# The first weight sum of the last feed-forward product in a tile of the larger pool, a third tile finished by an accumulating store, and the last tile's gain product in two parts

## The chip, the cores and the metric

One core of a Trainium2 chip (trn2). The metric is the time of one execution on the device in microseconds (us); lower is better. Engines are named as the profile names them: PE (TensorE matmul) and PEld (its weight load), DVE (VectorE), ACT (ScalarE), POOL (GpSimd), SP (SyncE, which here only issues transfers).

## What is computed

One decoder layer over 1,024 tokens and 16 meta tokens, width 1,024, all in float32. The change lies in the last third of it, the feed-forward block and its norm:

```python
u = rmsnorm(h, g_pre_ffn[l])
f = jnp.square(jax.nn.relu(u @ w_ff1[l])) @ w_ff2[l]
h = h + rmsnorm(f, g_post_ffn[l])
return h[:, N_META:]
```

Here h is [1024, 1024] without the meta tokens, w_ff1 is [1024, 4096], w_ff2 is [4096, 1024], and rmsnorm(x, g) is x / sqrt(mean(x^2) + 1e-6) * g. Ahead of it stand the input projection, sliding-window attention, a linear recurrence and the output projection; the change leaves them alone.

## The kernel before

**Products in three matmuls.** To keep float32 accuracy each operand is split into a high part (a copy rounded by ACT, line 95) and a low part (source minus high part, by DVE, line 98). Each block product is then three matmuls: high times high (line 123), high times low (line 124), low times high (line 125), all accumulated in the same bank of PSUM. A tile of 128x1024 elements thus costs one ACT instruction and one DVE instruction before PE may use it.

**Seven products in place of eight.** Both feed-forward products are done in a Strassen-Winograd form: sums and differences of blocks on DVE or in transfers, seven block products in place of eight. For the second feed-forward matmul the list PLAN holds the seven products, i = 0 to 6. Each is done in eight steps q = 0 to 7 over the 4,096 hidden rows, and a step (i, q) needs one weight tile (128x1024, from one or two blocks of w_ff2) and one activation tile, both split. In each step PE runs 4 row tiles j times 6 matmuls. The seventh product (i = 6) is the last one; its weight is the sum of two blocks of w_ff2 and its activation is the difference of two activation blocks. Its row tile j = 3 is computed in two halves of 256 columns, in two PSUM banks. The last three steps (q = 5, 6, 7) are held back and run row tile by row tile at the end, so that the tiles j = 0, 1, 2, 3 are finished one after the other.

**Two ways of a weight sum.** `fetch_2` loads the blocks. Either both blocks come by plain loads on SP's queue (line 1058) and DVE adds them in `prep_2`, or the first comes by a plain load and the second by an accumulating transfer issued by POOL (line 1055), which adds it to the tile in flight. For i = 6 the list LASTW says, for each q, from which pool the tile comes and whether the second block has a tile of its own (a name) or is accumulated (None). The accumulated ones are q = 0, 2, 3, 5, 7.

**Pools.** A pool is a set of tiles that are given out again once all readers of the former content are done; a transfer into such a tile waits for them. "raw" and "e" have 2 tiles each and hold weights as loaded; "ws" has 4 (split weights); "b" has 17 (split activations, sums of activations, and, until product 5 is over, four result tiles); "a" has 16.

**Queues.** Every engine takes its instructions in the order of its own queue. A scheduler writes that order when the program is built, with a timing model of its own. POOL's queue holds few things: the accumulating transfers, and the powers -1/2 of a norm (`rstd_of`, lines 160 to 164: DVE writes ms, POOL raises it to -1/2 as rs at line 164, DVE multiplies by rs).

**The end.** The output tiles 4 to 7 (results "1", j = 0 to 3) are complete after product 5 and are finished by `finish_early` during the end of product 5 and the start of product 6: squares on ACT, ms, rs, one DVE instruction (line 1124), and a store on POOL that accumulates onto the residual already standing in the output (line 1128). The output tiles 0 to 3 are finished by `finish_half` and `finish_late`. For j = 0 and 1 the way is the same as in `finish_early` (squares of the last half on ACT, line 1117; ms; rs; line 1158; accumulating store, line 1162). For j = 2 and 3 the sum of squares is taken by DVE (line 1165), rs by POOL (line 1173), the product with the gain g by DVE (line 1175, the first half earlier at line 1145), and the residual, loaded ahead by SP (line 1143), is added by DVE together with the factor rs (line 1177); two plain stores by SP and ACT follow (line 1180).

Of the kernel before, what the change touches and what calls it, by code (L numbers as in the profile page):

```python
# [9 lines left out]
F32 = mybir.dt.float32  # L10
F32R = mybir.dt.float32r
AF = mybir.ActivationFunctionType
ALU = mybir.AluOpType
# [3 lines left out]
P = 128  # L17
# [20 lines left out]
def hybrid_layer(  # L38
# [6 lines left out]
    nc = tc.nc  # L45
# [4 lines left out]
    small = ctx.enter_context(tc.tile_pool(name="small", bufs=4))  # L50
# [7 lines left out]
    def slot(tag, shape, dt=F32):  # L58
        uid[0] += 1
        return slab.tile(shape, dt, tag=tag, name=f"{tag}{uid[0]}", bufs=bufs[tag])  # L60
# [44 lines left out]
    def behind(name, *inss):  # L105
        for ins in inss:
            tc.add_manual_dep(
                ins, name,
                mybir.DependencyInfo(
                    mybir.DependencyClass.NoSync, mybir.DependencyReason.DATA  # L110
                ),
                reason="order",
            )
# [38 lines left out]
    half_pow = const.tile([P, 1], F32, name="half_pow")  # L152
    nc.gpsimd.memset(half_pow, -0.5)

    def rstd_of(ssq_parts, n=P):
        ms = small.tile([P, 1], F32, name="ms", tag="ms")
        if len(ssq_parts) == 1:
            nc.gpsimd.tensor_scalar(ms[:n], ssq_parts[0], EPS, None, op0=ALU.add)
        else:
            nc.vector.scalar_tensor_tensor(  # L160
                ms[:n], ssq_parts[0], EPS, ssq_parts[1], op0=ALU.add, op1=ALU.add
            )
        rs = small.tile([P, 1], F32, name="rs", tag="rs")
        nc.gpsimd.tensor_tensor(rs[:n], ms[:n], half_pow[:n], op=ALU.pow)  # L164
        return rs[:n]
# [251 lines left out]
    for b in range(2):  # L417
        pv = bank("pt", (P, 4, P))
        for i in range(4):
            o = NMETA + (4 * b + i) * P  # L420
# [366 lines left out]
    def combine(dst, x0, x1, op):  # L787
        return nc.vector.tensor_tensor(dst, x0, x1, op=op).ins  # L788
# [227 lines left out]
    def product_by_parts(acc, w, op):  # L1016
# [22 lines left out]


    LASTW = [
        ("raw", None), ("e", "raw"), ("b", None), ("b", None), ("raw", "e"), ("b", None),
        ("e", "raw"), ("b", None),
    ]

# [67 lines left out]
    COLS = (slice(0, 512), slice(512, 1024))  # L1113

    def squares(sq, src, n):
        p_ = small.tile([P, 1], F32, name=f"sq{n}", tag=f"sq{n}")
        nc.scalar.activation(sq, src, AF.Square, scale=RMS_SC, accum_out=p_)
        return p_
# [13 lines left out]
    def finish_half(j):  # L1132

        o = slot("a", [P, D])
        acc, c = facc["0", j], COLS[1]
        ssq = small.tile([P, 1], F32, name=f"late{j}", tag=f"late{j}", bufs=1)
        nc.scalar.activation(
            o[:, c], acc[:, c], AF.Square, scale=RMS_SC, accum_out=ssq
        )
        h = None  # L1140
        if j > 1:
            h = slot("d", [P, D])
            nc.sync.dma_start(h, out[j * P : (j + 1) * P, :])
            nc.gpsimd.tensor_scalar(ssq, ssq, EPS, None, op0=ALU.add)
            behind(w_low[0], combine(o[:, c], acc[:, c], gffn_b[:, c], ALU.mult))
        halves[j] = h, o, ssq

    def finish_late(j, y, parts):

        h, o, ssq = halves[j]  # L1150
        acc = facc["0", j]
        for k, c in enumerate(parts):
            yield k
            ins = combine(acc[:, c], y[k], acc[:, c], ALU.add)
            if k == 1:
                behind(w_low[0], ins)
            if j < 2:
                w_low[0] = nc.vector.scalar_tensor_tensor(
                    o, acc, rstd_of([squares(o[:, c], acc[:, c], 0), ssq]), gffn_b,
                    op0=ALU.mult, op1=ALU.mult,  # L1160
                ).ins.name
                nc.gpsimd.dma_start(out[j * P : (j + 1) * P, :], o, accum_op=ALU.add)
                continue
            part = small.tile([P, 1], F32, name=f"part{k}", tag=f"part{k}")
            nc.vector.tensor_tensor_reduce(
                out=o[:, c], in0=acc[:, c], in1=acc[:, c], scale=RMS_SC * RMS_SC,
                scalar=ssq, op0=ALU.mult, op1=ALU.add, accum_out=part,
            )
            ssq = part
        if j < 2:  # L1170
            return
        rs = small.tile([P, 1], F32, name="rs", tag="rs")
        nc.gpsimd.tensor_tensor(rs, ssq, half_pow, op=ALU.pow)
        c = COLS[0]
        combine(o[:, c], acc[:, c], gffn_b[:, c], ALU.mult)
        for c, eng in zip(COLS[::-1], (nc.sync, nc.scalar)):
            w_low[0] = nc.vector.scalar_tensor_tensor(
                o[:, c], o[:, c], rs, h[:, c], op0=ALU.mult, op1=ALU.add
            ).ins.name
            eng.dma_start(out[j * P : (j + 1) * P, c], o[:, c])  # L1180
# [37 lines left out]
    for n, (i, q) in enumerate(steps):  # L1218
        while fetched < min(n + (4 if n < 45 else 6), len(steps)):
            raw_2[fetched] = fetch_2(fetched)  # L1220
            fetched += 1
        if n + 1 < len(steps):
            late = w_low[0]
            ready[n + 1] = prep_2(n + 1, "a" if n + 1 >= len(steps) - LAST else "ws")
        if q == 0:
            old = None if i == 0 else accs
            accs = [[bank(("acc", "s", "pt", "o")[j])] for j in range(4)]
            if i == 6:

                evict(5, 0, old[0][0], late)  # L1230
                accs[3] = [accs[3][0][:, :256], bank("acc")[:, :256]]
        if n < len(steps) - LAST:
            for j in range(4):
                for acc, cols in zip(accs[j], col_parts(i, j)):
                    step_mm(acc, j, q, ready[n], cols)
            del ready[n]
        if old and (q > 0 or i < 6) and q < 4:
            evict(i - 1, q, old[q][0], late)
        if i == 5 and q == 0:
            gffn_b = slot("a", [P, D])  # L1240
            nc.scalar.dma_start(gffn_b, g_post_ffn[0].partition_broadcast(P))
        if (i, q) in EARLY:
            finish_early(EARLY.index((i, q)))
        if i == 6 and 1 <= q < 5:
            finish_half(q - 1)
    for j in range(4):
        parts = col_parts(6, j)
        for k in finish_late(j, accs[j], parts):
            for n in sorted(ready):
                step_mm(accs[j][k], j, steps[n][1], ready[n], parts[k])  # L1250
# [31 lines left out]
```

## Time and profile before

| | us |
|---|---|
| median of 3 runs | 973.48 (972.43 to 975.89) |
| the profiled execution's own time | 972.95 |
| span of its profile, first to last instruction | 971.1 |
| mean granted clock of TensorE in it | 0.999 of full speed |

Times inside the span are counted from its start. A row of the timeline gives the start, the length of one instruction, the engine, the line of the kernel, the operation, what it writes and reads, and in brackets how long the engine was idle before it and what ended that. In the chain of work that ended last, each row is a start, a length and what the time was spent on; "issue" is time in which the engine waited for nothing that the profile shows. In the DMA view the last number of a row is the median time from issue to landing. Sums, differences and products of two tiles go through the helper `combine` and stand at its line 788. A window of the timeline may start with an instruction that began just before it.

### The profile page before, as it was taken

The page shows a single profiled execution, that of the slowest core. Times are in us where ns is not written, and L with a number is a line of the kernel's source. Part 1 is how long each engine was busy: PE and PEld are TensorE (multiplying, and loading weights), DVE is VectorE, ACT ScalarE, POOL GpSimd, SP SyncE. Part 2 cuts the span into 40 slices and gives each one's busy share as a digit, 9 for nine tenths or more (in the row PEclk, how much of TensorE's full clock was granted, in tenths as well). Part 3 has the DMA queues.
Part 4 walks back from the last instruction along what each step waited for, and adds up shares of the span by engine and source line. Part 5 has one row for each costly group of instructions (what it writes and reads, how often), then busy time and mean ns, then how long its engine had stood idle before and what let it go on. Part 6 is the DMA issues. An engine that isn't in the chain of part 4 may idle for free.

```text
span 971.1 us, 12490 instructions
## 1 busy us (share of the span) xinstructions
PE 953.7 (98%) x4782; PEld 803.0 (83%) x4782; DVE 674.6 (69%) x997; ACT 502.0 (52%) x809; POOL 82.4 (8%) x109
## 2 busy tenths in 40 slices
PE   6999999999999999999999999999999999999997
PEld 6999999888878887888888878888888888888786
DVE  6679997775976686665645465468557676779694
ACT  6646673567844554343555556555433344445350
POOL 4100000000002100000000000000111000003152
PEclk9999999999999999999999999999999999999999
DMA  9002001012234466576522264323678765548923
GB/s 296 23 1 66 23 23 44 23 48 64 84 119 144 159 207 209 173 251 209 198 87 87 97 206 125 114 87 114 172 176 198 186 224 187 184 163 195 223 80 87
DMA packets 88219, 130.13 MB, mean 134 GB/s; under 512 B 13624, under 2 KB 52552, under 8 KB 88160
## 3 DMA queue, kind: packets, MB, share of 16 engines
q1 hardware_dynamic: 79792, 107.33, 33.4%
q0 software_dynamic: 7792, 20.45, 10.1%
q10 hardware_dynamic: 576, 1.57, 0.4%
q8 instruction: 37, 0.61, 0.2%
q14 instruction: 22, 0.18, 0.1%
HBM read 110.46 MB, written 18.87 MB: 133 GB/s over the span
## 4 chain that ended last, share of the span: by engine, by line
PE 89%; DVE 4%; DMA 3%; issue 2%; ACT 1%; POOL 0%; SPq 0%; POOLq 0%; DVEq 0%; ACTq 0%
PE ps_acc L124 11%; PE ps_acc L123 11%; PE ps_acc L125 11%; PE ps_s L125 6%; PE ps_pt L123 6%; PE ps_s L124 6%; PE ps_pt L125 6%; PE ps_s L123 6%; PE ps_pt L124 6%; PE ps_o L124 5%; PE ps_o L123 5%; PE ps_o L125 5%; PE ps_o L506 2%; PE ps_pt L495 1%; DMA raw<-in_w_ff_dram 1%
## 5 line engine op out<-in xcount | busy, mean ns | idle before, releaser
L95 ACT CAST ws<-raw 128x1024 fp32r<-128x1024 f32 (+1 forms) x69 | 70.7, 1024 | 126.6 <-PE ps_o L124 48.8
L98 DVE TENSOR_TENSOR ws<-raw,ws 128x1024 fp32r<-128x1024 f32 (+1 forms) x70 | 83.5, 1194 | 59.6 <-ACT ws L95 59.5
L123 PE MATMUL ps_acc<-a,ws 128*128 128x256 f32 (+2 forms) x272 | 90.5, 333 | 0.6 <-DVE b L305 0.6
L124 PE MATMUL ps_acc<-a,ws 128*128 128x256 f32 (+2 forms) x272 | 89.8, 330 | 0.0
L125 PE MATMUL ps_acc<-a,ws 128*128 128x256 f32 (+2 forms) x272 | 89.4, 329 | 0.0
L98 DVE TENSOR_TENSOR b<-b,b 128x1024 fp32r<-128x1024 f32 (+2 forms) x48 | 57.6, 1201 | 24.7 <-PE ps_o L124 17.1
L95 ACT CAST ws<-e 128x1024 fp32r<-128x1024 f32 x43 | 45.0, 1046 | 55.3 <-PE ps_o L124 28.1
L95 ACT CAST b<-b 128x1024 fp32r<-128x1024 f32 (+2 forms) x48 | 49.4, 1030 | 42.8 <-DVE b L788 40.0
L98 DVE TENSOR_TENSOR ws<-e,ws 128x1024 fp32r<-128x1024 f32 x43 | 52.6, 1222 | 21.6 <-ACT ws L95 21.6
L123 PEld LDWEIGHTS ps_acc<-a,ws 128*128 128x128 f32 x272 | 51.2, 188 | 4.9 <-DVE b L305 0.8
L125 PEld LDWEIGHTS ps_acc<-a,ws 128*128 128x128 f32 x272 | 51.2, 188 | 4.6
L124 PEld LDWEIGHTS ps_acc<-a,ws 128*128 128x128 f32 x272 | 51.2, 188 | 3.9
L164 POOL TENSOR_TENSOR rs<-ms,half_pow 128x1 f32<-128x1 f32 (+1 forms) x31 | 21.3, 692 | 356.5 <-DVE ms L160 355.1
L123 PE MATMUL ps_acc<-ws,b 128*128 128x512 f32 (+1 forms) x120 | 46.3, 386 | 0.4 <-ACT ws L95 0.4
L124 PE MATMUL ps_acc<-ws,b 128*128 128x512 f32 (+1 forms) x120 | 46.5, 388 | 0.2 <-DVE ws L98 0.2
L125 PE MATMUL ps_acc<-ws,b 128*128 128x512 f32 (+1 forms) x120 | 46.2, 385 | 0.0
L123 PE MATMUL ps_pt<-ws,b 128*128 128x512 f32 x112 | 44.1, 394 | 0.0
L124 PE MATMUL ps_pt<-ws,b 128*128 128x512 f32 x112 | 44.1, 394 | 0.0
L125 PE MATMUL ps_pt<-ws,b 128*128 128x512 f32 x112 | 44.0, 393 | 0.0
L123 PE MATMUL ps_s<-ws,b 128*128 128x512 f32 x110 | 43.4, 395 | 0.0
L124 PE MATMUL ps_s<-ws,b 128*128 128x512 f32 x110 | 43.3, 393 | 0.0
L125 PE MATMUL ps_s<-ws,b 128*128 128x512 f32 x110 | 43.3, 393 | 0.0
(381 smaller groups left out, 2690.1 us busy)
## 6 DMA issues: line engine op xcount, KB each, us to landing
raw<-in_w_ff_dram SPq DMA_DIRECT2D x62, 512.0 KB, 4.0
e<-in_w_ff_dram SPq DMA_DIRECT2D x45, 512.0 KB, 3.6
d<-in_w_ff_dram SPq DMA_DIRECT2D x12, 512.0 KB, 3.8
s_dram<-d POOLq DMA_DIRECT2D x12, 512.0 KB, 3.9
raw<-in_w_in_dram SPq DMA_DIRECT2D x9, 512.0 KB, 3.6
c<-in_x_dram SPq DMA_DIRECT2D x8, 512.0 KB, 8.5
d<-in_x_dram SPq DMA_DIRECT2D x8, 512.0 KB, 4.6
out_dram<-raw SPq DMA_DIRECT2D x8, 512.0 KB, 2.6
```

What stands on the lines that cost most here:

```text
L95: nc.scalar.copy(hi, src)
L98: low = nc.vector.tensor_tensor(lo, src, f32(hi), op=ALU.subtract).ins
L123: nc.tensor.matmul(dst, lh, rh, start=start, stop=False, skip_group_check=True)
L124: nc.tensor.matmul(dst, lh, rl, start=False, stop=False, skip_group_check=True)
L125: nc.tensor.matmul(dst, ll, rh, start=False, stop=stop, skip_group_check=True)
L164: nc.gpsimd.tensor_tensor(rs[:n], ms[:n], half_pow[:n], op=ALU.pow)
L495: nc.tensor.transpose(pt[:, o : o + P], sn[h][:, 2 * bp + i, s * P : (s + 1) * P], ident,)
L506: nc.tensor.matmul(po[:, oc : oc + n], v, p_[:, pc : pc + n], start=first and k == 0, stop=last and k == 1, skip_group_check=True,)
```

## The change

Three edits. First, the weight tile of step (6, 0), the first weight sum of the last product, comes from the pool "b" and no longer from "raw"; it is still loaded by SP and then accumulated by POOL. Second, output tile 2 is finished as tiles 0 and 1 are (ACT squares, line 1158, accumulating store on POOL), so its residual is no longer loaded. Third, for tile 3 the product with g of the last 512 columns is made in two parts of 256 columns, inside the loop over the parts.

```diff
     LASTW = [
-        ("raw", None), ("e", "raw"), ("b", None), ("b", None), ("raw", "e"), ("b", None),
+        ("b", None), ("e", "raw"), ("b", None), ("b", None), ("raw", "e"), ("b", None),
         ("e", "raw"), ("b", None),
     ]
...
         h = None
-        if j > 1:
+        if j > 2:
             h = slot("d", [P, D])
...
-            if j < 2:
+            if j < 3:
                 w_low[0] = nc.vector.scalar_tensor_tensor(
...
             ssq = part
-        if j < 2:
+            if k == 1:
+                rs = small.tile([P, 1], F32, name="rs", tag="rs")
+                nc.gpsimd.tensor_tensor(rs, ssq, half_pow, op=ALU.pow)
+            combine(o[:, c], acc[:, c], gffn_b[:, c], ALU.mult)
+        if j < 3:
             return
-        rs = small.tile([P, 1], F32, name="rs", tag="rs")
-        nc.gpsimd.tensor_tensor(rs, ssq, half_pow, op=ALU.pow)
-        c = COLS[0]
-        combine(o[:, c], acc[:, c], gffn_b[:, c], ALU.mult)
```

The scheduler writes the queues anew. POOL's queue around the first weight sums, in the order of the two programs (the names are ours: sum q is the accumulating transfer of step (6, q); rs 7 and store 7 belong to output tile 7):

```
before: store 6, sum 2, rs 7, sum 3, store 7, sum 0, sum 5, sum 7
after:  store 6, sum 0, sum 2, rs 7, store 7, sum 3, sum 5, sum 7
```

On SP's queue, before: the plain load of sum 2, e (step (5, 7)), of sum 3, of sum 0, e, of sum 5, raw. After: the plain load of sum 0, e (step (5, 7)), of sum 2, of sum 3, raw, e, of sum 5, raw. On DVE's queue the order from the activations of step (5, 0) up to the end of product 6 is the same, but for one early product with g that is gone; at the very end, tile 2's line 1158 stands between tile 3's first addition of a PSUM bank (line 1154) and tile 3's first sum of squares, and tile 3's first product with g stands behind the addition of its second bank and ahead of the second sum of squares.

## The prediction

> **What bounds the kernel now.** I read the page first, then the chain of waits over the last 130 us, then the timelines of POOL, DVE and PE there.
>
> ```profile
> PE 953.7 (98%) x4782; PEld 803.0 (83%) x4782; DVE 674.6 (69%) x997; ACT 502.0 (52%) x809; POOL 82.4 (8%) x109
> PE 89%; DVE 4%; DMA 3%; issue 2%; ACT 1%; POOL 0%; SPq 0%; POOLq 0%; DVEq 0%; ACTq 0%
> ```
>
> PE is the bound: busy 98%, 89% of the chain. The change leaves its matmuls as they are, so it can only move PE's waits and the tail behind its last matmul. Near the edit the chain leaves PE:
>
> ```profile
> 889.74 5.08 DMA b<-in_w_ff_dram
> 894.86 6.88 issue
> 901.78 0.62 POOL b L1055
> ...
> 903.91 3.76 issue
> 907.68 9.19 DMA raw<-in_w_ff_dram
> 916.96 1.05 ACT ws L95
> 918.03 1.24 DVE ws L98
> 919.31 0.50 PE ps_acc L124
> ```
>
> Read upwards: PE waited for the split of the first weight sum (raw), whose accumulating transfer was issued only at 907.68. PE's rows give the price:
>
> ```profile
> 917.25 0.40 PE L125 MATMUL ps_o<-ws,b 128*128 128x512 f32 x1
> ...
> 918.39 0.40 PE L123 MATMUL ps_s<-ws,b 128*128 128x512 f32 x1
> 918.62 0.40 PE L123 MATMUL ps_pt<-ws,b 128*128 128x512 f32 x1
> 918.86 0.28 PE L123 MATMUL ps_o<-ws,b 128*128 128x256 f32 x1
> 919.31 0.50 PE L124 MATMUL ps_acc<-ws,b 128*128 128x512 f32 x1 [0.18 <-DVE ws L98]
> 919.65 0.40 PE L125 MATMUL ps_acc<-ws,b 128*128 128x512 f32 x1
> ```
>
> Undisturbed starts lie 0.23 apart for 512 columns (918.39 to 918.62) and half of it for 256. From 917.25 to 919.65 there should be five times 0.23 and one 0.12, 1.27; there are 2.40. The stall costs 1.13 us, and that is all that the first edit can gain.
>
> **Why was that sum late?** POOL's timeline:
>
> ```profile
> 890.11 0.89 POOL L1128 DMA_DIRECT2D out_dram<-a  x1 [2.53 <-DVE a L1124]
> 892.44 1.21 POOL L1055 DMA_DIRECT2D b<-in_w_ff_dram  x1 [1.44 <-issue]
> 893.19 1.45 POOL L164 TENSOR_TENSOR rs<-ms,half_pow 128x1 f32<-128x1 f32 x1
> 901.75 1.23 POOL L1055 DMA_DIRECT2D b<-in_w_ff_dram  x1 [7.11 <-PE ps_o L125]
> 902.51 1.41 POOL L1128 DMA_DIRECT2D out_dram<-a  x1
> 907.68 1.22 POOL L1055 DMA_DIRECT2D raw<-in_w_ff_dram  x1 [3.77 <-issue]
> 917.20 1.20 POOL L1055 DMA_DIRECT2D b<-in_w_ff_dram  x1 [8.29 <-issue]
> ```
>
> The DMA view over 892.4 to 892.9, then over 901.7 to 902.4, tells when two of these sums landed:
>
> ```profile
> b<-in_w_ff_dram POOLq DMA_DIRECT2D x1, 512.0 KB, 9.0
> b<-in_w_ff_dram POOLq DMA_DIRECT2D x1, 512.0 KB, 5.6
> ```
>
> 892.44 + 9.0 = 901.4, and the next sum starts at 901.75; 901.75 + 5.6 = 907.35, the next starts at 907.68; 907.68 + 9.19 = 916.87, the next at 917.20. Each sum starts 0.3 us after the one before it has landed, though its own plain load was long there (889.74 + 5.08 = 894.82 for the one issued at 901.75). So two sums are never in flight together, and POOL stands still meanwhile: the store at 902.51 stood behind such a sum. PE named at 901.75 is not the cause; the chain calls that time "issue". A store beside a sum is let through (902.51 behind 901.75).
>
> [...]
>
> **The change, part by part.** *The first sum.* It takes the place of sum 2: its plain load goes out where that of sum 2 did, and its accumulation at 892.44 as the first of the five. It lands by 901.4 and is due at 918.29 (917.25 + 4 x 0.23 + 0.12, the low part's first use). Gain: 1.13. Sums 2, 3, 5 and 7 follow in the four later places; sum 2 is then accumulated from 901.75 on, and its split on ACT, the first to read it, is not near:
>
> ```profile
> 926.86 1.04 ACT L95 CAST ws<-b 128x1024 fp32r<-128x1024 f32 x1
> ```
>
> So none of the later sums becomes the new late one; sum 3 lands where sum 0 landed before (916.87) and is used one step behind sum 2.
>
> *What the edit moves.* In the new order of POOL, sum 2 stands ahead of rs 7; before, rs 7 ran at 893.19, in the shadow of the first sum. Sum 2 can't start until the first sum has landed, so rs 7 waits behind it, and DVE's queue holds line 1124 of output tile 7, which needs rs 7, ahead of the low part of step (5, 5):
>
> ```profile
> 873.51 0.56 POOL L164 TENSOR_TENSOR rs<-ms,half_pow 128x1 f32<-128x1 f32 x1 [105.40 <-DVE ms L160]
> 874.10 1.29 DVE L1124 SCALAR_TENSOR_TENSOR a<-b,rs,a 128x1024 f32<-128x1024 f32 x1 [0.68 <-POOL rs L164]
> 875.30 1.22 DVE L98 TENSOR_TENSOR ws<-e,ws 128x1024 fp32r<-128x1024 f32 x1
> 895.27 1.28 DVE L1124 SCALAR_TENSOR_TENSOR a<-b,rs,a 128x1024 f32<-128x1024 f32 x1
> 896.46 1.22 DVE L98 TENSOR_TENSOR ws<-e,ws 128x1024 fp32r<-128x1024 f32 x1
> 901.77 0.39 PE L124 MATMUL ps_acc<-ws,b 128*128 128x512 f32 x1
> ```
>
> The first three rows are output tile 4's, where DVE did wait for rs; the last three are the place in question. Sum 2 starts at 901.75; rs 7 0.75 later, as 893.19 after 892.44: 902.50; 0.56 for it while DVE stands still: 903.06; line 1124 at 903.09; the low part 1.20 later (874.10 to 875.30): 904.29; its end, 1.22 on: 905.51; PE 0.04 later (918.03 + 1.24 to 919.31): 905.55. Before, PE used it at 901.77. Loss 3.78, and 0.11 for the restart (919.31 to 919.65 is 0.34, not 0.23): 3.9 us. Net of the 1.13: +2.8.
>
> *When the first sum lands.* The plain load of sum 2 now goes out right behind e, near 887.6, one more 512 KB transfer ahead of that landing, while transfers fill the time:
>
> ```profile
> 884.00:902.00 18.00, 18.00 (x80) 14.66 (x79) 16.05 (x18) 8.01 (x10) 5.68 (x6) 1.00 0.98 247
> ```
>
> At a DMA share of 0.98 and 247 GB/s (last two columns) 524 kB take 2.1 us. Two loads of before that start near 898 (e, sum 5) now wait for the blocked DVE and make room. Bounds 0 and 2.1; I take 1.0, the middle, as both lie within those 18 us. [...]
>
> *What else DVE owes.* From line 1124 on DVE runs 7.8 late (903.09 for 895.27), but before it idled on the way:
>
> ```profile
> 901.90 1.23 DVE L98 TENSOR_TENSOR ws<-raw,ws 128x1024 fp32r<-128x1024 f32 x1 [1.95 <-ACT ws L95]
> 908.85 1.22 DVE L98 TENSOR_TENSOR ws<-e,ws 128x1024 fp32r<-128x1024 f32 x1
> 918.03 1.23 DVE L98 TENSOR_TENSOR ws<-raw,ws 128x1024 fp32r<-128x1024 f32 x1 [5.57 <-ACT ws L95]
> ```
>
> The low part of step (5, 7) (second row) was ready at 908.85 + 1.22 = 910.07; a step is 24 times 0.23, so it was due near 901.77 + 2 x 5.55 = 912.9, 2.8 early. Now it is 7.8 - 1.95 = 5.9 late, and PE itself is 3.9 late: 2.8 + 3.9 - 5.9 leaves 0.8. In front of the first sum's low part (third row) DVE idled 5.57 more, which goes too: it stays ready in time. So one stall, not two.
>
> *The tail.* Tile 3's end, behind PE's last matmul (963.72 + 0.28 = 964.00):
>
> ```profile
> 964.19 0.42 DVE L788 TENSOR_TENSOR a<-ps_acc,a 128x256 f32<-128x256 f32 x1
> 964.65 0.49 DVE L1165 CUSTOM_DVE_ANT_0 a<-a,part 128x256 f32<-128x256 f32 x1
> 966.31 1.41 DVE L1177 SCALAR_TENSOR_TENSOR a<-a,rs,d 128x512 f32<-128x512 f32 x2 [0.44 <-POOL rs L1173]
> out_dram<-a POOLq DMA_DIRECT2D x2, 512.0 KB, 5.1
> ```
>
> DVE's rows 964.19 and 964.65 are the addition of the last bank and the sum of squares that needs it; the first part of the product with g (256 columns, the size of the addition's 0.42) now stands between them. The gap of 0.46 already holds some waiting of the second for the first, which that part fills: +0.1 to +0.4. The second part lies under POOL's power, as all of it did before; taking half away gains nothing there. Tile 2 loses two instructions like the last DVE row (1.42) and gains one like line 1124's 1.28: even. Its store now goes out on POOL, by my estimate about when PE ends (964), and takes 5.1 (last row, the stores of tiles 0 and 1): about 969, before the span's 971.1 but beside tile 3's two stores. I take +0.5 for the tail, bounds 0 and 1.5. One 512 KB load of SP's disappears from far earlier, under PE: nothing.
>
> **Sum.** +2.8 + 1.0 + 0.5 = +4.3 us, bounds +2.8 and +6.4. The profiled execution's own 972.95 becomes 977.25; the median of the runs shown, 973.48, becomes 977.8, which I predict.
>
> **The rivals.**
> 1. *POOL does not stand still*: sums overlap, rs 7 runs on time. Then -1.13 + 0.5 = -0.6: 972.9, no change. It decides if rs 7 starts before 898.7: 901.77 less 0.56 for rs, 0.03, 1.20, 1.22 and 0.04. Against it: every row of line 1055 quoted, the one behind the other's landing each time. For it: POOL's rows are 1.2 us long, not 9, so the wait itself is only inferred from the gaps. [...] Chance 0.10.
> 2. *A second stall*: the 0.8 us left for step (5, 7) is too little, because the first sum lands over 1 us later than taken or ACT's splits slip. Another 1 to 2: +6.3, 979.8. Chance 0.10.
> 3. *Cover that I don't see* (rs 7 sooner, the landing earlier, ACT and DVE closing up): +1 to +2.8, about 975.5. Chance 0.15.
> Forecast: 0.65. That the change does not do what it says (the first sum no earlier) is ruled out by POOL's new order, where it leads.
>
> **Range.** The forecast's bounds, 976.3 to 979.9, less and plus what one side of the runs shown allows (973.48 - 972.43 = 1.0), reach 975.3 to 980.9; with the third rival 975.0 to 980.7. About 0.3% (2.9 us) is what a measurement of this kernel can tell from no change. Slower by more than that: most of the forecast (0.58 of 0.65), rival 2, a little of rival 3: 0.71. Within: rival 1, most of 3, the forecast's low end: 0.26. Faster: 0.03, as no more than 1.13 can be won.
>
> **What would show it.** Right: rs 7 near 902 to 904 in POOL's timeline, line 1124 of tile 7 idle before it by some 7 us with POOL as its releaser, a PE stall of 4 to 5 us near 902 at line 124, none near 918. Wrong: two rows of line 1055 closer than 5 us; rs 7 near 893; a PE stall of more than 1 us elsewhere; tile 3's stores over 1.5 us later behind PE's last matmul.

## The result and the profile after

| | us |
|---|---|
| before, median of 6 runs | 974.41 (972.43 to 976.29) |
| after, median of 6 runs | 979.38 (978.78 to 979.94) |
| ratio, 95% interval | 1.0049 (1.0034 to 1.0064) |
| profiled execution of after: own time, span, mean granted clock | 979.05, 977.2, 0.994 |

The change makes the kernel slower by 5.0 us. The forecast was 977.8 with a range up to 980.7. That is close, but two of its terms were wrong, in opposite directions, as the runs below show.

POOL's timeline of after (start, length, engine, line, what it writes and reads, idle time before):

```profile
892.43 1.21 POOL L1055 DMA_DIRECT2D b<-in_w_ff_dram  x1 [1.49 <-issue]
902.38 1.22 POOL L1055 DMA_DIRECT2D b<-in_w_ff_dram  x1 [8.73 <-issue]
903.13 1.05 POOL L164 TENSOR_TENSOR rs<-ms,half_pow 128x1 f32<-128x1 f32 x1
906.14 0.90 POOL L1128 DMA_DIRECT2D out_dram<-a  x1 [1.95 <-issue]
908.55 1.23 POOL L1055 DMA_DIRECT2D b<-in_w_ff_dram  x1 [1.51 <-issue]
```

The first row is now sum 0; the DMA view gives its time to landing:

```profile
b<-in_w_ff_dram POOLq DMA_DIRECT2D x1, 512.0 KB, 9.6
```

It lands at 892.43 + 9.6 = 902.0, and sum 2 (second row) starts 0.3 us later, after 8.73 us in which POOL did nothing. rs 7 (third row) stands behind it and starts at 903.13; before, it ran at 893.19. DVE's timeline shows who needed it:

```profile
894.01 1.22 DVE L788 TENSOR_TENSOR b<-b,a 128x1024 f32<-128x1024 f32 x1
904.22 1.29 DVE L1124 SCALAR_TENSOR_TENSOR a<-b,rs,a 128x1024 f32<-128x1024 f32 x1 [8.98 <-POOL rs L164]
905.42 1.22 DVE L98 TENSOR_TENSOR ws<-e,ws 128x1024 fp32r<-128x1024 f32 x1
```

DVE waited 8.98 us at line 1124 of output tile 7, with the low part of step (5, 5) next in its queue. PE's view of waits from 880 on has a single row, and its timeline shows the price:

```profile
PE ps_acc L124 <- DVE ws L98: 4.8, 1, 4.8
```

```profile
901.47 0.39 PE L123 MATMUL ps_o<-ws,b 128*128 128x512 f32 x1
906.69 0.79 PE L124 MATMUL ps_acc<-ws,b 128*128 128x512 f32 x1 [4.83 <-DVE ws L98]
907.28 0.63 PE L125 MATMUL ps_acc<-ws,b 128*128 128x512 f32 x1
907.71 0.63 PE L123 MATMUL ps_acc<-ws,b 128*128 128x512 f32 x1
...
910.70 0.63 PE L125 MATMUL ps_s<-ws,b 128*128 128x512 f32 x1
911.12 0.45 PE L124 MATMUL ps_pt<-ws,b 128*128 128x512 f32 x1
911.42 0.39 PE L125 MATMUL ps_pt<-ws,b 128*128 128x512 f32 x1
911.64 0.39 PE L123 MATMUL ps_pt<-ws,b 128*128 128x512 f32 x1
```

The step from 901.47 to 906.69 is 5.22 where 0.23 would be normal: the stall is 5.0. Then comes something the prediction did not have. The starts lie 0.43 apart, not 0.23, up to 911.12. From 906.69 to 911.42 are eleven steps in 4.73 us; eleven of 0.23 take 2.53. That is 2.2 us more. A table by window (start:end, length, busy time of PE, PEld, DVE, ACT, POOL, then the granted clock, DMA share, GB/s) names the cause:

```profile
901.50:904.40 2.90, 0.36 (x2) 0.00 (x0) 0.18 (x1) 0.30 (x1) 1.81 (x2) 1.00 0.14 9
904.40:911.23 6.83, 4.54 (x11) 3.57 (x12) 6.83 (x7) 1.05 (x1) 2.13 (x2) 0.50 0.91 176
911.23:914.00 2.77, 2.77 (x14) 2.25 (x13) 1.66 (x3) 1.58 (x2) 0.00 (x0) 1.00 1.06 293
```

The granted clock was 0.50 for 6.83 us: 2.29 of it over the idle time (904.40 to 906.69), the other 4.54 over the ten slow matmuls.

The stall near 918 is gone. At the end, DVE and POOL run as follows behind PE's last matmul, which ends at 969.49:

```profile
969.53 0.42 DVE L788 TENSOR_TENSOR a<-ps_acc,a 128x256 f32<-128x256 f32 x1
969.87 0.41 DVE L788 TENSOR_TENSOR a<-a,a 128x256 f32<-128x256 f32 x1
970.20 0.48 DVE L1165 CUSTOM_DVE_ANT_0 a<-a,part 128x256 f32<-128x256 f32 x1
...
970.72 0.42 DVE L788 TENSOR_TENSOR a<-a,a 128x256 f32<-128x256 f32 x1
971.61 1.42 DVE L1177 SCALAR_TENSOR_TENSOR a<-a,rs,d 128x512 f32<-128x512 f32 x2 [0.46 <-POOL rs L1172]
```

```profile
969.56 0.89 POOL L1162 DMA_DIRECT2D out_dram<-a  x1 [1.93 <-issue]
970.84 0.73 POOL L1172 TENSOR_TENSOR rs<-part,half_pow 128x1 f32<-128x1 f32 x1 [0.39 <-DVE part L1165]
```

From PE's end to line 1177 it takes 2.12 us (before: 966.31 - 964.00 = 2.31), from line 1177 to the end of the span 977.2 - 971.61 = 5.6 (before: 971.1 - 966.31 = 4.8). Tile 2's store (969.56, 5.3 to landing) is now in flight beside tile 3's two.

### The profile page after: what moved, and what is told of

The parts are those of the page before. It is cut to its first block, busy times and chain, and to the rows that moved or that the text cites. A ratio compares the mean times of both kernels' runs of the same rounds, so it can differ in the third digit from the quotient of the medians.

```text
span 977.2 us, 12480 instructions
## 1 busy us (share of the span) xinstructions
PE 954.3 (98%) x4782; PEld 803.3 (82%) x4782; DVE 672.9 (69%) x994; ACT 503.2 (51%) x811; POOL 75.3 (8%) x109
## 5 line engine op out<-in xcount | busy, mean ns | idle before, releaser
L95 ACT CAST ws<-raw 128x1024 fp32r<-128x1024 f32 (+1 forms) x68 | 69.6, 1024 | 119.3 <-PE ps_o L124 47.9
L98 DVE TENSOR_TENSOR b<-b,b 128x1024 fp32r<-128x1024 f32 (+2 forms) x48 | 57.6, 1200 | 25.9 <-PE ps_o L124 18.4
```

The costliest lines, as they stand in the source:

```text
L95: nc.scalar.copy(hi, src)
L98: low = nc.vector.tensor_tensor(lo, src, f32(hi), op=ALU.subtract).ins
```

## The experiments

Each kernel was timed against the kernel before on the same chip, in five rounds; the last two runs are single profiles.

**One part of the change at a time.** The first edit alone:

```diff
-        ("raw", None), ("e", "raw"), ("b", None), ("b", None), ("raw", "e"), ("b", None),
+        ("b", None), ("e", "raw"), ("b", None), ("b", None), ("raw", "e"), ("b", None),
```

> Only the first edit (the first weight sum of the last product in a tile of the larger pool); the end is that of before. Theory (rs 7 stands behind sum 2 in POOL's queue, sum 2 waits for the first sum's landing): the PE stall near 902 is there in full, rs 7 at 902 to 904, ten matmuls behind it 0.43 apart in place of 0.23, the stall near 918 gone; some 4.4 us above before, that is the 5.0 measured less 0.6 for the end. Rival (the two edits at the end carry the loss): 1 us below before, no stall near 902.

Measured: 978.59 (977.55 to 981.35), before 974.0, ratio 1.0049 (1.0034 to 1.0064). POOL, PE, and a window:

```profile
903.77 1.22 POOL L1055 DMA_DIRECT2D b<-in_w_ff_dram  x1 [8.49 <-issue]
904.53 1.05 POOL L164 TENSOR_TENSOR rs<-ms,half_pow 128x1 f32<-128x1 f32 x1
```

```profile
908.09 0.80 PE L124 MATMUL ps_acc<-ws,b 128*128 128x512 f32 x1 [4.66 <-DVE ws L98]
```

```profile
908.10:911.51 3.41, 3.41 (x8) 2.73 (x9) 3.41 (x4) 1.05 (x1) 1.56 (x2) 0.50 1.05 184
```

The loss comes with this edit: the same wait, and again half clock, here for one stretch of 3.41 us and eight matmuls, where ten were expected. rs 7 came a little later than the 902 to 904 expected, since this execution had already lost 1.6 us near 775 (more of that wait below).

The second and third edit alone (tile 2 by an accumulating store, the product with g in two parts, as in the change's diff):

> Only the second and the third edit (tile 2 finished by an accumulating store, tile 3's product with g in two parts); the weight sums as before. Theory: no stall near 902, the stall of 1.1 us near 918 stays, the end some 0.6 us longer behind PE's last matmul: 0.3 to 0.8 us above before, hardly to be told from it. Rival (the end carries the loss): 4 to 5 us above before.

Measured: 975.25 (972.42 to 977.86), ratio 1.0007 (0.9996 to 1.0019). No wait near 902. But the old stall was far larger in this profile than in the one the prediction used:

```profile
920.15 0.50 PE L123 MATMUL ps_acc<-ws,b 128*128 128x512 f32 x1 [2.76 <-ACT ws L95]
...
921.41 0.50 PE L124 MATMUL ps_acc<-ws,b 128*128 128x512 f32 x1 [0.17 <-DVE ws L98]
```

```profile
918.60:922.03 3.43, 1.72 (x7) 1.21 (x8) 1.90 (x2) 1.99 (x2) 1.20 (x1) 1.00 0.26 21
922.03:925.44 3.41, 3.41 (x10) 2.64 (x9) 3.41 (x5) 1.66 (x3) 0.02 (x1) 0.50 1.02 220
```

2.76 + 0.17 of waiting, and half clock for 3.41 us, which set in 1.9 us after PE had started again. The weights of the first sum come the same way here as in the kernel before, so the old stall is not a fixed 1.1 us. The last two runs come back to this.

**Is POOL held by a lack of room for the transfers?** The changed kernel with one constant larger. That it is room for descriptors was my theory; the runs show what the constant does to the times, not what fills it:

```diff
-        "TRN2", target_bir_lowering=False, num_devices=1, dynamic_dma_scratch_size=1024
+        "TRN2", target_bir_lowering=False, num_devices=1, dynamic_dma_scratch_size=1536
```

> The changed kernel with 1536 in place of 1024 bytes for the descriptors of POOL's transfers (dynamic_dma_scratch_size), all queues in the same order. Theory (an accumulating load is held until the one before it has landed because there is no room for its descriptors): sum 2 starts within 2 us of sum 0, rs 7 before 897, no PE stall near 902, none near 918: 973.9, that is 974.4 less 1.1 for the old stall and plus 0.6 for the end. Rival (POOL's wait has another cause: a semaphore, the plain load, or a limit of one accumulating load in flight): sum 2 still 0.3 behind sum 0's landing, 979.4 as the changed kernel.

Measured: 972.09 (970.68 to 973.27), ratio 0.9979 (0.997 to 0.9988). POOL's timeline:

```profile
889.61 1.46 POOL L1055 DMA_DIRECT2D b<-in_w_ff_dram  x1
893.91 1.20 POOL L1055 DMA_DIRECT2D b<-in_w_ff_dram  x1 [2.84 <-DMA b<-in_w_ff_dram]
894.66 1.03 POOL L164 TENSOR_TENSOR rs<-ms,half_pow 128x1 f32<-128x1 f32 x1
```

Sum 0 takes 11.2 us to land here (DMA view), to 900.8; sum 2 goes out at 893.91, 6.9 us before that, as soon as its own plain load is there (4.3 us behind sum 0, where at most 2 were expected). rs 7 runs at 894.66, and PE has no wait after 880. What kept two sums apart was this constant: at 1,536 bytes two were in flight together, at 1,024 sum 2 started 0.3 us after the landing of sum 0. How much of it one such sum takes was not measured.

**Is rs 7's place in POOL's queue the cause?** The changed kernel with 1,024 bytes, and rs 7 ahead of sum 2 (last_rs holds the last instruction of line 164, held the sum that is put off):

```diff
-                nc.gpsimd.dma_start(raws[0], w2v[q, a, b], accum_op=ADD)
+                held.append((raws[0], w2v[q, a, b])); (i, q) == (6, 2) or nc.gpsimd.dma_start(*held.pop(), accum_op=ADD)
...
-    EARLY = [(5, 3), (5, 5), (5, 7), (6, 1)]
+    EARLY = [(5, 3), (5, 5), (5, 7), (6, 0)]
...
-            finish_early(EARLY.index((i, q)))
+            finish_early(EARLY.index((i, q))); (i, q) == (6, 0) and behind(last_rs[0], nc.gpsimd.dma_start(*held.pop(), accum_op=ADD).ins)
```

> The changed kernel with one swap in POOL's queue: rs 7 stands ahead of sum 2 (the finishing of tile 7 is written one step earlier, and sum 2 is ordered behind its rs); the other queues keep their order. Theory: sum 2 still starts at 901.7 to 902.5, behind sum 0's landing, but rs 7 runs near 894 and DVE is not held; no PE stall near 902 nor near 918: 973.9. Rival (the sums themselves are late, or the larger pool is short of tiles, whatever stands between them): a stall of several us stays, 977 to 979.

Measured: 971.68 (970.68 to 974.16), ratio 0.998 (0.997 to 0.999).

```profile
894.58 1.21 POOL L1055 DMA_DIRECT2D b<-in_w_ff_dram  x1 [1.37 <-issue]
895.38 1.41 POOL L164 TENSOR_TENSOR rs<-ms,half_pow 128x1 f32<-128x1 f32 x1
904.42 1.23 POOL L1243 DMA_DIRECT2D b<-in_w_ff_dram  x1 [7.63 <-issue]
```

Sum 2 (here on line 1243) still starts only 9.84 us behind sum 0, after 7.63 us in which POOL did nothing, but nobody waits for POOL meanwhile, and PE has no wait after 880. Both this kernel and the one before it came out some 2 us below what was expected of them. That is the first sign that the old stall was worth more than 1.1. The one execution of this kernel that was profiled, at 974.16, was its slowest, and lost time well ahead of the change:

```profile
776.07 0.50 PE L124 MATMUL ps_acc<-ws,b 128*128 128x512 f32 x1 [1.49 <-DVE ws L98]
```

Such a wait, for a low part of weights in product i = 2, stands near 757 or 775 in five of the ten profiles of kernels with 1,024 bytes (0.3 to 1.6 us) and in none of the four with 1,536. No edit touches that place; the cause was not traced. It shifts everything behind it, here sum 2 to 904.42 where 901.7 to 902.5 was expected.

**Is it DVE's order that carries the wait to PE?** The changed kernel with one exchange in DVE's queue, the low part of step (5, 5) ahead of line 1124 of tile 7:

```diff
+        low_55[0] = w_low[0] if (i, q) == (5, 5) else low_55[0]
...
-        nc.vector.scalar_tensor_tensor(
+        ins = nc.vector.scalar_tensor_tensor(
             o, acc, rstd_of(ssq), gffn_b, op0=ALU.mult, op1=ALU.mult
-        )
+        ).ins
+        j == 3 and behind(low_55[0], ins)
```

> The changed kernel with one exchange in DVE's queue and nothing else: the low part of step (5, 5) stands ahead of line 1124 of output tile 7, not behind it. Theory (the loss is the low part that stands behind an instruction waiting for rs 7): rs 7 still starts near 903 behind sum 2 and line 1124 still near 904.2, but the low part runs near 895 and PE has no stall near 902. What stands behind line 1124 now is what step (5, 6) needs: three DVE instructions of 1.14 each after 905.4, so its low part ends near 908.9 where it is due near 907.3: a stall of 0 to 1.7 us there, too short for the clock to fall (a stall of 1.1 in the kernel before left it at 1.0). Time about 972.5 to 975.5, against 979.4 of the changed kernel. Rival (rs 7 late holds PE by another way, the store or a tile that is not free): a stall of 4 to 5 us near 902 stays, 979.

Measured: 975.19 (974.03 to 976.0), before 974.32, ratio 1.0008 (0.9998 to 1.0019). DVE, then PE (line numbers from 1072 on are one or two higher in this kernel):

```profile
895.91 1.22 DVE L98 TENSOR_TENSOR ws<-e,ws 128x1024 fp32r<-128x1024 f32 x1 [1.04 <-ACT ws L95]
903.64 1.28 DVE L1125 SCALAR_TENSOR_TENSOR a<-b,rs,a 128x1024 f32<-128x1024 f32 x1 [6.50 <-POOL rs L164]
...
907.11 1.22 DVE L98 TENSOR_TENSOR ws<-raw,ws 128x1024 fp32r<-128x1024 f32 x1
```

```profile
908.38 0.50 PE L124 MATMUL ps_acc<-ws,b 128*128 128x512 f32 x1 [1.33 <-DVE ws L98]
...
915.33 0.50 PE L124 MATMUL ps_acc<-ws,b 128*128 128x512 f32 x1 [1.16 <-DVE ws L98]
```

DVE waits for rs 7 as long as ever, yet the 5 us are gone. Two waits of 1.3 and 1.2 are left, one step apart; the first was expected, the second was not. The prediction's own sum has it: the 0.8 us that it left for step (5, 7) counted on PE being 3.9 late, and here PE is only some 1.5 late. The clock stayed at 1.00 in every window of 5 us from 895 to 930. The kernel is 4.2 us faster than the changed one by an exchange of two instructions.

**What do the end edits cost?** The first edit with rs 7 ahead of sum 2 (the diff above without the end edits); then the same with the third edit, here for tile 2 as well, which keeps its plain stores:

```diff
             ssq = part
+            if k == len(parts) - 1:
+                rs = small.tile([P, 1], F32, name="rs", tag="rs")
+                nc.gpsimd.tensor_tensor(rs, ssq, half_pow, op=ALU.pow)
+            combine(o[:, c], acc[:, c], gffn_b[:, c], ALU.mult)
         if j < 2:
             return
-        rs = small.tile([P, 1], F32, name="rs", tag="rs")
-        nc.gpsimd.tensor_tensor(rs, ssq, half_pow, op=ALU.pow)
-        c = COLS[0]
-        combine(o[:, c], acc[:, c], gffn_b[:, c], ALU.mult)
```

> The first edit with rs 7 ahead of sum 2 in POOL's queue, and without the second and third edit. Theory (the two end edits cost 0.5 us, in the landing of tile 3's stores beside tile 2's): from the end of PE's last matmul to the end of the span 7.1 us as in the kernel before, not 7.7 to 7.9 as with the end edits; no PE wait after 880; time about 971.2, 0.5 below the kernel that has the end edits as well (971.7). Rival (the end edits are even, the 0.6 is scatter of one profile): 971.7, and the stretch behind the last matmul 7.5 or more here too.

> As the kernel without the end edits, but with the product with g of the last 512 columns made in two parts (for tile 3; tile 2 keeps its plain stores). Theory: DVE's chain from the last addition to line 1177 stays at 2.1 us and the stores land in 2.6, so the stretch behind the last matmul is 7.1 as without the edit: the price of the end edits is tile 2's accumulating store alone. Rival (the split product costs or gains): the chain from the last addition to line 1177 differs from 2.1 by over 0.2 us.

Measured: 971.61 (970.31 to 972.74), ratio 0.997 (0.9958 to 0.9982); and 970.96 (970.37 to 971.52), ratio 0.9967 (0.9955 to 0.9979). The medians don't separate the edits, the profiles do. PE's last matmul and line 1177 of the first, then of the second:

```profile
962.65 0.28 PE L125 MATMUL ps_acc<-a,b 128*128 128x256 f32 x1
```

```profile
965.24 1.41 DVE L1177 SCALAR_TENSOR_TENSOR a<-a,rs,d 128x512 f32<-128x512 f32 x2 [0.44 <-POOL rs L1173]
```

```profile
961.32 0.28 PE L125 MATMUL ps_acc<-a,b 128*128 128x256 f32 x1
```

```profile
963.84 1.41 DVE L1177 SCALAR_TENSOR_TENSOR a<-a,rs,d 128x512 f32<-128x512 f32 x2 [0.44 <-POOL rs L1172]
```

From PE's end to line 1177: 2.31, and 2.24 with the third edit. From line 1177 to the end of the spans (970.0 and 968.6): 4.8 in both, where the changed kernel has 5.6. So tile 2's accumulating store costs 0.8 us at the very end, and the third edit gains 0.1.

**How much is the old stall worth?** The kernel before with 1,536 bytes and nothing else (the constant above):

> The kernel before with 1,536 bytes of descriptor room for POOL's transfers in place of 1,024, and no other change. Theory (the old late sum was late only because POOL was held): sum 0 goes out by 905 and lands by 914, PE has no wait near 918, time 971.5 to 972.9 (1.1 to 2.5 us less than before). Rival (sum 0 is late for other reasons: its plain load, or sum 3 ahead of it): it still lands after 916, a stall of about 1 us stays, 974.

Measured: 971.22 (970.75 to 972.34), before 974.32, ratio 0.9969 (0.9958 to 0.998).

```profile
902.46 1.21 POOL L1055 DMA_DIRECT2D raw<-in_w_ff_dram  x1 [4.04 <-DMA raw<-in_w_ff_dram]
```

Sum 0 goes out at 902.46, not 907.68, and PE has no wait after 880. The gain is 3.1 us, more than the range expected. Two more with 1,536 bytes, first with the third edit, then with the first edit as well:

> The kernel before with 1,536 bytes of descriptor room and the third edit alone (the last tile's product with g in two parts); the first weight sum stays in the smaller pool. Theory: with the room no PE wait is left after 880, and the third edit takes 0.1 us off the end: 971.1, ratio 0.996 to 0.997. Rival (what more room brought was the chance of one series): 972.5 or more.

> The same with the first edit as well. Theory: with the room neither the old stall nor the new one exists, so the place of the first sum no longer matters: 971.1, equal to the kernel without the first edit within 0.4. Rival (the first edit still gains, since the first sum's landing varies): 0.5 to 1 less, 970.3.

Measured: 971.2 (970.75 to 971.61), ratio 0.9965 (0.9953 to 0.9978); and 971.12 (970.57 to 971.68), ratio 0.9965 (0.9951 to 0.9978). With 1,536 bytes, no difference between the two places of the first sum can be seen. These and the kernel at 970.96 are the fastest found; they can't be told apart.

**Does the old stall vary?** The kernel before, unchanged, profiled twice more:

> The kernel before, unchanged, profiled again. Theory (its stall near 918 varies between executions, since the first sum's landing is the sum of three transfers in a row; the one profile shown had a short one): sum 0 is issued between 907 and 911, PE's wait near 918 to 921 is anywhere from 1 to 4 us, at 2.8 and more with half clock after it; the profiled time less the wait and the half clock's loss is 971 to 972.5. Rival (the stall is 1.1 each time and the rest of the spread lies elsewhere): a wait of 1.0 to 1.3 again, whatever the time.

> The same once more: theory, the wait near 918 to 921 differs from the other two profiles by over 0.3 us and the time moves with it; rival, 1.0 to 1.3 again.

Measured: 973.52 and 974.84. The waits of PE from 880 on, in the first and in the second:

```profile
919.74 0.50 PE L124 MATMUL ps_acc<-ws,b 128*128 128x512 f32 x1 [0.18 <-DVE ws L98]
```

```profile
919.87 0.50 PE L123 MATMUL ps_acc<-ws,b 128*128 128x512 f32 x1 [1.54 <-ACT ws L95]
...
921.13 0.50 PE L124 MATMUL ps_acc<-ws,b 128*128 128x512 f32 x1 [0.18 <-DVE ws L98]
```

The waits are 0.18 in one, 1.72 in the other, 0.58 in the first profile of before, 2.93 with the end edits alone. They vary, but the 0.18 lies under the 1 to 4 us expected, and the times less the waits (973.3 and 973.1) lie over the 971 to 972.5 expected. That is because the brackets hold only the time in which PE is idle. PE's time from the start of step (5, 6) (906.39 in the first profile of before) to the end of its last matmul tells more. It is 55.9 to 56.0 in all nine profiles without the old stall and without a stall in that stretch, the changed kernel's among them, and 57.6, 57.2 and 58.8 in the three of before. So the old stall cost 1.6, 1.2 and 2.8 there, and 5.1 with the end edits alone, half clock included. The three times less these costs are 971.3 to 972.3, as expected.

The cost follows the first sum, which stands last in a row of three transfers that each start when the one before has landed (0.3 us behind it, in the prediction's rows): in the three profiles it landed 10.5, 10.2 and 11.6 us after the start of step (5, 6), with the end edits alone 12.8. In none of the three did the clock fall while PE was at work; 1.72 of waiting did not bring half clock, 2.93 did.

## Why the prediction came out near, and which steps were wrong

**The mechanism held, step by step.** POOL stands still until a sum has landed (8.73 us), rs 7 stands behind sum 2 (forecast 902 to 904, measured 903.13), line 1124 waits for it and the low part of step (5, 5) waits behind line 1124. Each link was cut by itself: the constant of 1,024 bytes, rs 7's place, DVE's order. Each time the stall of 5 us went. The stall was forecast at 3.8 for the order plus 1.0 for the sum's landing and 0.1 for the restart, 4.9; it measured 5.0. Inside it two errors balance: sum 0 landed 0.6 later than sum 2 did before (902.0 against 901.4), not 1.0, and rs 7 took 1.05, not the 0.56 of the row that I took. The row at 893.19, which like rs 7 now ran right behind a sum, took 1.45 and was the nearer one.

**The sum lacked the clock: +2.2.** The prediction priced the stall as idle time alone. After it, ten matmuls ran at half clock. No row of before near the change showed a clock under 1, but the end of before did, behind PE's last matmul (964.00):

```profile
964.00:968.20 4.20, 0.00 (x0) 0.00 (x0) 3.21 (x8) 0.00 (x0) 0.99 (x1) 1.00 0.49 166
968.20:971.10 2.90, 0.00 (x0) 0.00 (x0) 0.00 (x0) 0.00 (x0) 0.00 (x0) 0.50 0.40 150
```

There the granted clock was 0.50 from 4.2 us after PE had stopped, and a forecast stall of 4.9 us is longer. So the cost was left out, at nothing, without a reason.

**"All that the first edit can gain" was wrong twice.** The 1.13 was read from rows that end at 919.65. In the steps behind it PE restarted late three times more, by 0.1 to 0.2 us, so that the old stall cost 1.6 in that very execution. Profile against profile the sum then reads 972.95 - 1.6 + 5.0 + 2.2 + 0.6 = 979.15, measured 979.05; the forecast had 977.25 there, 1.8 too little. And the old stall varies, and the profiled execution had one of the shorter. In the five kernels that have neither of the two stalls nor the second edit, the median lies 2.7 to 3.4 us under that of before (3.1 with 1,536 bytes alone). How much of that is the old stall is not fully shown: it was 1.2 to 2.8 in the three profiles of before. With 3.1 the sum by the medians reads 974.4 - 3.1 + 5.0 + 2.2 + 0.6 = 979.1, measured 979.4.

The sum was made against the profile and then carried over to the median as it stood. By the medians the two misses, 2.2 too little loss and 2.0 too little gain, nearly cancelled. That the net came out near was luck, and not the sum's being right. (Also, the range ends at 980.7, where its own bounds reach 980.9; nothing hangs on that.)

**The tail: size right, parts not.** Forecast +0.5, measured +0.6 (7.7 for 7.1 behind PE's last matmul). The +0.1 to +0.4 on DVE was wrong in sign: the chain to line 1177 is 0.2 shorter. The first part of the product does delay the sum of squares (from the addition to it 0.67, before 0.46), but beside the shorter second part POOL's power ends sooner (0.73 long, before 0.99), as the last section shows for another run. The loss, 0.8, is all in the landing of the last stores, which the prediction had named.

**The rivals.** "POOL does not stand still" falls by the 8.73 us and by the runs with 1,536 bytes, where they are gone: the rows are 1.21 us long, as it says, but at 1,024 bytes the next sum starts only 0.3 us after the landing of the one before. The second stall did not come in the changed kernel; it came, at 1.2 us, when the first was shortened by the exchange on DVE. Its time, 979.8, was nearer than the forecast's all the same, by the half clock and not by its mechanism. The unseen cover wasn't there.

## What to carry to other kernels

When an edit shifts one transfer in an in-order queue, list the small instructions that now stand behind it and who waits for them: here one power of 128 numbers cost 7 us, and an exchange of two instructions in POOL's queue, or 512 bytes more in one constant, took it away. Price a stall of TensorE that is several microseconds long with half clock behind it (here 3.41 to 6.83 us of it came with waits of 2.93 to 4.83). And where the runs of a kernel scatter by 4 to 6 us (before, in its four series) and those of kernels without one of its waits by 0.9 to 3.5, don't take the price of that wait from a single profile, nor from the idle time in its brackets: count from one instruction ahead of it to the end, cut the wait, and time what is left.

## What the runs showed of the hardware

**Half clock came in stretches of 3.41 us and of twice that.** Near the change it lasted 6.83, 3.41 and 3.41 us in the three kernels where it came. It set in 2.5 us after PE had stopped in the changed kernel, 4.7 us after in the first edit alone, and with the end edits alone when PE had been at work again for 1.9 us. There 2.93 of waiting were enough, and in the 3.43 us ahead of that fall PE was busy for 1.72. Two waits of 1.3 and 1.2, and one of 1.72, did not bring it.

**At 1,024 bytes an accumulating transfer waits for the landing of the one before.** With 1,024 bytes, the next sum starts 0.3 us after that landing; with 1,536, it went out 6.9 us ahead of it. Meanwhile POOL's queue stands still (8.73 us in the changed kernel), and the profile calls the time "issue" (there) or names a releaser that is not the cause (PE, for 7.11 us at 901.75 in before).

**POOL's power ends later beside a longer DVE product.** POOL's rs of the last tile and DVE's product beside it, in the kernel before and in the one with rs 7 first and the third edit:

```profile
965.18 0.69 DVE L788 TENSOR_TENSOR a<-a,a 128x512 f32<-128x512 f32 x1
965.29 0.99 POOL L1173 TENSOR_TENSOR rs<-part,half_pow 128x1 f32<-128x1 f32 x1 [2.87 <-DVE part L1165]
```

```profile
962.98 0.42 DVE L788 TENSOR_TENSOR a<-a,a 128x256 f32<-128x256 f32 x1
963.09 0.72 POOL L1172 TENSOR_TENSOR rs<-part,half_pow 128x1 f32<-128x1 f32 x1 [3.07 <-DVE part L1165]
```

It is 0.27 us shorter, exactly by what DVE's product beside it is shorter (0.69 and 0.42), and ends 0.41 us behind it both times. POOL's instruction is the same in both (128x1); why it is longer in the first was not shown.
